# Differential attention with one transposed group split out of PSUM by two engines, a new order of steps, and two small edits in the windowed attention

## The chip, the cores and the metric

The kernel runs on one core of a Trainium2 chip. TensorE (PE; PEld are its weight loads), VectorE (DVE), ScalarE (ACT), GpSimd (POOL) and SyncE (SP, which here only issues DMAs) each run their own instructions in program order and meet through semaphores. The metric is the time of one execution on the device in microseconds (us); lower is better.

## The reference, cut to what matters

One inference step of a two-layer network over 128 context tokens and 1024 latent tokens, all float32. Layer 0 mixes tokens by differential attention, layer 1 by windowed grouped attention with a sink. Each is followed by an output projection and a feed-forward network.

```
# layer 0, latent tokens: 8 heads, 1024 queries, 256 cached + 1024 keys = 1280
s = einsum('bqhmd,bkhmd->bhmqk', q, k) * scale        # m = 0, 1: two score maps per head
p = softmax(s, axis=-1)
a = p[:, :, 0] - lam * p[:, :, 1]
o = einsum('bhqk,bkhe->bqhe', a, v)
# layer 1: 16 heads, blocks of 128 queries, 256 context keys + up to 384 neighbours
s_lat = where(|q_pos - k_pos| <= 128, s_lat, -1e30)
m = maximum(max(s), sink);  e = exp(s - m)
p = e / (sum(e) + exp(sink - m))
```

## The kernel before, in words

**Number format.** Products that need float32 accuracy are made of two rounded halves (float32r): `hi` is the rounded value and `lo` the remainder, and three matmuls (hi hi, hi lo, lo hi) stand for one.

**Differential attention** (`diff_attention`) works on 32 *pairs*: a pair is one head and two blocks of 128 queries (i = 0, 1). Per block and score map m there are 1280 scores. Their way through the engines is cut into steps, each named by a letter:

- S: scores on PE into a PSUM tile (L737, two such tiles). R: row maximum on DVE (L744). E: exponential with row sum on ACT (L749).
- c: the factor of the second map on DVE, a reciprocal (L755) and a product of three columns (L756). C: the combination of both maps, 128x1280, on DVE (L761).
- T: transposes on PE (L768), in groups g = 0, 1, 2 of 4, 4 and 2 blocks of 128 keys, into the one PSUM tile `tpa` (its slot is shared with `tpo`). V: ACT copies the group to SBUF (L773). P: POOL rounds it (`pool_round`, L110) and subtracts the rounded value from it (L784).
- A: products with V on PE (L793 to L795). X, B, Y: the result is copied, transposed back (L806), copied and written to `o_d` (L812).
- W: every other pair, a piece of the output weights is loaded and split on ACT (L102) and DVE (L103).
- l, s, n: loads, statistics and scaling for the first tiles of the output projection that follows (L1253, L1263 and L1275 on ACT).

The order is written out by hand. `ROUND` is a list of tokens run once per pair; a token's letter is the step, its first digits are (g or m, i), and its last digit says how many pairs back it acts. Each engine runs its own instructions in the order in which the tokens emit them. `DRAIN` finishes the last pairs.

**Second attention** (`swa_attention`) has units of one group of four heads and 128 queries. Per head: scores (L1014, L1017, and L1020, which adds the mask by a matmul with the identity), maximum (L1025), its minimum with the negated sink (L1026), exponential (L1029). At its start the mask is loaded by DMA into `mraw` and cast by ACT (L987), and the identity is cast (L989).

Of the kernel before, what the change touches and what calls it, by code (L numbers as in the profile page):

```python
# [9 lines left out]
F32 = mybir.dt.float32  # L10
F32R = mybir.dt.float32r
BF16 = mybir.dt.bfloat16
AF = mybir.ActivationFunctionType
ALU = mybir.AluOpType
# [4 lines left out]
P = 128  # L19
# [25 lines left out]
def hybrid_step(ctx: ExitStack, tc: tile.TileContext, x_prompt, x_sample, cache_diff_k, cache_diff_v,  # L45
# [38 lines left out]
    subg = const.tile([P, 1], F32, name="subg")  # L84
    neglam = const.tile([P, 1], F32, name="neglam")
    negsink = const.tile([P, SH], F32, name="negsink")

    def sbuf(name, side=None):
        return tc.tile_pool(name=name, bufs=1, side=side, reuse_waits="tile")
# [351 lines left out]

    def small_params(sb):

        dma(out=subg, in_=diff_subln_g.rearrange("o p -> p o"))
        act.mul(out=subg, in_=subg, mul=1.0 - LAM_INIT)
        lp = sb.tile([P, 4, HD], F32, name="lp")
        dma(out=lp, in_=diff_lambda.rearrange("o f d -> o (f d)").broadcast_to([P, 4 * HD]).rearrange(
            "p (f d) -> p f d", d=HD))
        lpp = sb.tile([P, 2, HD], F32, name="lpp")
        dve.tensor_tensor(out=lpp, in0=lp[:, 0:4:2, :], in1=lp[:, 1:4:2, :], op=ALU.mult)  # L450
        le = sb.tile([P, 2], F32, name="le")
        dve.tensor_reduce(out=le, in_=lpp, axis=AX.X, op=ALU.add)
        act.activation(out=le, in_=le, func=AF.Exp)
        dve.tensor_tensor(out=neglam, in0=le[:, 1:2], in1=le[:, 0:1], op=ALU.subtract)
        dve.tensor_scalar(out=neglam, in0=neglam, scalar1=-LAM_INIT, scalar2=None, op0=ALU.add)
        dma(out=negsink, in_=swa_sink.broadcast_to([P, SH]))
        act.mul(out=negsink, in_=negsink, mul=-1.0)
# [258 lines left out]
    def diff_attention(op, s1_all, wo_pool, pre, kv0, q0):  # L716
        NKB = NCB + 8
        NK = NKB * P
        with sbuf("da") as sb, psum("dap") as ps:
            class Pair:  # L720
# [31 lines left out]
                def step_c(self, _, i):  # L752

                    r = self.s2[i][:, 1:2]
                    dve.reciprocal(out=r, in_=self.s2[i][:, 0:1])  # L755
                    dve.scalar_tensor_tensor(out=r, in0=self.s1(i), scalar=neglam, in1=r, op0=ALU.mult, op1=ALU.mult)  # L756

                def step_C(self, _, i):

# [4 lines left out]
                def step_T(self, g, i):  # L764

                    tp = self.tp[i, g] = ps.tile([P, 4, P], F32, name="tpa", tag="t", bufs=1)
                    for t in range(4 * g, min(4 * g + 4, NKB)):
                        pe.transpose(tp[:, t - 4 * g, :], self.a[i][:, t * P:(t + 1) * P], ident)  # L768

                def step_V(self, g, i):  # L770
                    n = min(4, NKB - 4 * g)
                    x = self.a32[i, g] = sb.tile([P, 4, P], F32, name="a32", tag="a32", bufs=2)
                    act.copy(out=x[:, 0:n, :], in_=self.tp[i, g][:, 0:n, :])  # L773

                def step_P(self, g, i):

                    n = min(4, NKB - 4 * g)
                    if g not in self.aT:
                        self.aT[g] = sb.tile([P, 2, 4 if g < 2 else 2, 2 * P], F32R, name="aT",
                                             tag="aT" if g < 2 else "aTb", bufs=4 if g < 2 else 2)  # L780
                    hi, lo = [self.aT[g][:, f, 0:n, i * P:(i + 1) * P] for f in range(2)]
                    x = self.a32[i, g][:, 0:n, :]
                    pool_round(hi, x)
                    (dve if self.last else pool).tensor_tensor(out=lo, in0=x, in1=hi.bitcast(F32), op=ALU.subtract)  # L784
# [34 lines left out]
            def wo_piece(i):  # L819
# [5 lines left out]

            ROUND = ("c001 A003 T012 A003 V202 V102 S000 R111 P213 T112 P002 A003 A003 E011 A003 P202 V012 "
                     "C001 P102 E111 T212 R000 V112 W000 S100 P012 R100 T001 X003 A002 V212 c011 E000 A002 "
                     "A002 B003 S010 V001 C011 Y003 T201 R010 A002 P112 E100 A002 T101 S110").split()  # L830


            DRAIN = ("c001 l1 A003 A003 V202 P213 l0 T012 V102 R111 A003 A003 P002 E011 P202 V012 A003 "
# [3 lines left out]
                     "A001 A001 A001 A001 P211 A001 A001 A001 n0 s11 X001 B001 Y001 n1").split()  # L837
            n = len(pairs)

            def run(token, i):  # L840
# [139 lines left out]

    def swa_attention(op, wo_pool, pre, kv0, q0):
        with sbuf("sa") as sb, psum("sap") as ps:

            mask = sb.tile([P, 2, P], BF16, name="mask")
            mraw = sb.tile([P, 2, P], F32, name="mraw")
            dma(out=mraw, in_=swa_mask)
            act.copy(out=mask, in_=mraw)  # L987
            ident_b = sb.tile([P, P], BF16, name="ident_b")
            act.copy(out=ident_b, in_=ident)  # L989

            class Unit:


# [29 lines left out]
                def step_R(self, h):  # L1023
                    hs, nm = self.g * SG + h, self.nm[:, h:h + 1]
                    dve.tensor_reduce(out=nm, in_=self.S[h][:, self.c0:self.c1], axis=AX.X, op=ALU.max, negate=True)  # L1025
                    dve.tensor_tensor(out=nm, in0=nm, in1=negsink[:, hs:hs + 1], op=ALU.min)  # L1026

                def step_E(self, h):
                    act.activation(out=self.e[:, h, 0:self.nk], in_=self.S[h][:, self.c0:self.c1], func=AF.Exp,  # L1029
# [881 lines left out]
    f = la.f  # L1911
# [87 lines left out]
```

## Time and profile before

| | |
|---|---|
| median of 3 runs | 3180.54 us (3177.97 to 3180.6) |
| the profiled execution | 3179.54 us, span of its trace 3177.7 us |
| mean granted TensorE clock | 0.982 of full speed |
| busy share of the span | PE 94%, PEld 83%, DVE 65%, ACT 45%, POOL 38% |

The span runs from the first to the last traced instruction. The shares are means over stages with different limits: the differential attention lies at about 390 to 822 us, the second attention at about 1960 to 2230 us, and the feed-forward and projection stages fill most of the rest.

### The profile page before, as it was taken

Reading aid. Unit: us, or ns where it says so; the run is one execution under the profiler, and the core shown is the slowest. Engines: PE = TensorE matmul, PEld = TensorE weight load, DVE = VectorE, ACT = ScalarE, POOL = GpSimd, SP = SyncE. Lnnn points to the kernel's source line nnn. Section 1 sums busy time; section 2 is a strip of 40 time slices with the busy share of each in tenths; the row PEclk is TensorE's granted clock in tenths of the full one; section 3 lists DMA queues with packets and bytes.
Section 4 is the critical chain, followed back from the end, with each engine's and each line's share of the span. In section 5 each row is a group of like instructions: output and inputs, shape, how many; then the busy total and the mean of one; then the engine's idle time right before and its main releaser. Section 6 shows DMA issues by size and latency. Waiting matters only on the chain.

```text
span 3177.7 us, 47863 instructions
## 1 busy us (share of the span) xinstructions
PE 3000.0 (94%) x17998; PEld 2637.4 (83%) x17998; DVE 2070.7 (65%) x2849; ACT 1423.8 (45%) x2764; POOL 1215.6 (38%) x1120
## 2 busy tenths in 40 slices
PE   8999989988887999999999998999988999999999
PEld 5888777777776999999888787777768999998887
DVE  6786388888587777753786643999586633334544
ACT  6332267777554333333344323777443333333442
POOL 0453389999312444433000143666213434330000
PEclk9999999999898999999999999999999999999999
DMA  6675543332423343424865454433432322226664
GB/s 214 190 222 190 182 135 115 121 115 85 126 100 98 112 125 110 129 83 150 290 215 193 149 174 126 117 114 102 143 116 75 109 67 79 77 70 214 196 197 142
DMA packets 373807, 442.22 MB, mean 139 GB/s; under 512 B 26804, under 2 KB 295644, under 8 KB 373576
## 3 DMA queue, kind: packets, MB, share of 16 engines
q1 hardware_dynamic: 373576, 439.16, 43.9%
q8 instruction: 142, 2.33, 0.3%
q14 instruction: 89, 0.73, 0.1%
HBM read 335.71 MB, written 103.37 MB: 138 GB/s over the span
## 4 chain that ended last, share of the span: by engine, by line
PE 68%; POOL 13%; DVE 9%; ACT 4%; issue 3%; DMA 1%; SPq 1%; ACTq 0%; DVEq 0%; POOLq 0%
POOL aT L784 7%; PE guX L1516 6%; PE guX L1517 6%; PE guX L1518 6%; PE dacc L1633 6%; PE dacc L1635 6%; PE dacc L1634 6%; POOL aT L110 5%; PE qacc L556 4%; PE qacc L558 4%; PE qacc L557 4%; PE guY L1518 3%; PE guY L1516 3%; PE guY L1517 3%; PE guZ L1516 1%
## 5 line engine op out<-in xcount | busy, mean ns | idle before, releaser
L1633 PE MATMUL dacc<-fh,ahl 128*128 128x512 f32 x792 | 311.4, 393 | 2.4 <-DVE U L1552 2.4
L1635 PE MATMUL dacc<-fh,ahl 128*128 128x512 f32 x792 | 310.3, 392 | 0.0
L1634 PE MATMUL dacc<-fl,ahl 128*128 128x512 f32 x792 | 310.3, 392 | 0.0
L1549 POOL TENSOR_TENSOR sg<-sg,U 128x256 f32<-128x256 f32 x88 | 74.9, 851 | 576.2 <-ACT sg L1548 565.0
L556 PE MATMUL qacc<-whi,hh 128*128 128x512 f32 x648 | 259.3, 400 | 0.0
L558 PE MATMUL qacc<-whi,hl 128*128 128x512 f32 x648 | 254.3, 392 | 0.0
L557 PE MATMUL qacc<-wlo,hh 128*128 128x512 f32 x648 | 253.7, 391 | 0.6 <-DVE wlo L106 0.6
L617 POOL TENSOR_TENSOR qout<-t,t 128x512 f32<-128x512 f32 (+1 forms) x56 | 67.8, 1212 | 485.7 <-DVE vst L587 283.5
L784 POOL TENSOR_TENSOR aT<-a,aT 128x512 fp32r<-128x512 f32 x186 | 237.5, 1277 | 15.5
L1618 DVE TENSOR_TENSOR fl<-fraw,fh 128x1024 fp32r<-128x1024 f32 x132 | 161.7, 1225 | 118.6 <-ACT fh L1617 115.0
L744 DVE TENSOR_REDUCE nm<-S 128x1 f32<-128x1280 f32 x128 | 190.2, 1486 | 50.9 <-PE S L737 50.9
L1617 ACT CAST fh<-fraw 128x1024 fp32r<-128x1024 f32 x132 | 138.4, 1049 | 164.0 <-DMA fraw<-in_w_down_dram 157.4
L737 PE MATMUL S<-K,q 128*128 128x512 f32 (+1 forms) x768 | 184.5, 377 | 13.3 <-ACT e L749 9.2
L266 DVE SCALAR_TENSOR_TENSOR macc<-wmod,sc,macc 128x512 f32<-128x512 f32 x196 | 186.3, 994 | 0.0
L1633 PEld LDWEIGHTS dacc<-fh,ahl 128*128 128x128 f32 x792 | 148.7, 188 | 36.4 <-DVE U L1552 3.3
L1635 PEld LDWEIGHTS dacc<-fh,ahl 128*128 128x128 f32 x792 | 148.7, 188 | 33.5
L578 ACT CAST xT<-tpx 128x512 fp32r<-128x512 f32 x127 | 68.8, 591 | 240.2 <-issue 125.4
L1634 PEld LDWEIGHTS dacc<-fl,ahl 128*128 128x128 f32 x792 | 148.7, 188 | 32.8
L749 ACT ACTIVATE e<-S,nm 128x1280 f32<-128x1280 f32 x128 | 171.6, 1340 | 7.2 <-DVE nm L744 7.1
L737 PEld LDWEIGHTS S<-K,q 128*128 128x128 f32 x768 | 137.5, 193 | 44.3 <-ACT e L749 19.5
L110 POOL TENSOR_SCALAR aT<-a 128x512 fp32r<-128x512 f32 x192 | 154.2, 803 | 24.0 <-ACT a L773 24.0
L1488 DVE TENSOR_TENSOR fl<-fsum,fh 128x1024 fp32r<-128x1024 f32 x84 | 102.4, 1219 | 81.0 <-ACT fh L1486 81.0
(363 smaller groups left out, 9592.2 us busy)
## 6 DMA issues: line engine op xcount, KB each, us to landing
fraw<-in_w_down_dram SPq DMA_DIRECT2D x132, 512.0 KB
wmod<-in_w_mod_dram SPq DMA_DIRECT2D x112, 256.0 KB
araw<-a_d SPq DMA_DIRECT2D x132, 192.0 KB
fraw<-in_w_gate_dram SPq DMA_DIRECT2D x44, 512.0 KB
fraw<-in_w_up_dram SPq DMA_DIRECT2D x42, 512.0 KB
qT_d<-xT SPq DMA_DIRECT2D x36, 512.0 KB
q<-qT_d SPq DMA_DIRECT2D x64, 256.0 KB
wraw<-in_w_qkv_diff_dram SPq DMA_DIRECT2D x24, 512.0 KB
```

Of the source, the lines that this page charges most:

```text
L110: pool.tensor_scalar(out=out, in0=in_, scalar1=1.0, scalar2=0.0, op0=ALU.mult, op1=ALU.add)
L556: pe.matmul(acc, lhsT=xh, rhs=hi[:, a, :], start=(kb == 0), stop=False)
L557: pe.matmul(acc, lhsT=xh, rhs=lo[:, a, :], start=False, stop=False)
L558: pe.matmul(acc, lhsT=xl, rhs=hi[:, a, :], start=False, stop=(kb == KB - 1))
L737: pe.matmul(S[:, j:j + n], lhsT=self.q[:, f, m, i * P:(i + 1) * P], rhs=kv[self.h][0][:, m, j:j + n], start=(f == 0), stop=(f == 1))
L784: (dve if self.last else pool).tensor_tensor(out=lo, in0=x, in1=hi.bitcast(F32), op=ALU.subtract)
L1516: pe.matmul(o, lhsT=hi[:, kb, :], rhs=xh[:, kb, :], start=(first and kb == 0), stop=False, **more)
L1517: pe.matmul(o, lhsT=hi[:, kb, :], rhs=xl[:, kb, :], start=False, stop=False, **more)
L1518: pe.matmul(o, lhsT=lo[:, kb, :], rhs=xh[:, kb, :], start=False, stop=(kb == 3), **more)
L1633: pe.matmul(acc, lhsT=ah, rhs=hi[:, cs], start=(d == 0), stop=False)
L1634: pe.matmul(acc, lhsT=ah, rhs=lo[:, cs], start=False, stop=False)
L1635: pe.matmul(acc, lhsT=al, rhs=hi[:, cs], start=False, stop=(d == NDF - 1))
```

## The change

Four edits.

1. In the differential attention, the group g = 2 of block i = 1 (two transposed blocks, 256 columns) no longer goes through SBUF and POOL. ACT casts it from PSUM into `hi`, and DVE subtracts `hi` from the PSUM tile into `lo`. The other five groups of a pair are treated as before.
2. `ROUND` and `DRAIN` are new lists: the same steps in another order.
3. In step c, the product of three columns is a `tensor_scalar` with two column scalars instead of a `scalar_tensor_tensor`.
4. In the second attention, the minimum with the sink is a `tensor_scalar` with a column scalar instead of a `tensor_tensor`; the mask and the identity live in the constant pool and are made in `small_params`, during the first projection.

```diff
     def small_params(sb):
 
+        mraw = junk[:, 0:2 * P].rearrange("p (a k) -> p a k", k=P)
+        dma(out=mraw, in_=swa_mask)
+        act.copy(out=mask, in_=mraw)
+        act.copy(out=ident_b, in_=ident)
...
-                    dve.scalar_tensor_tensor(out=r, in0=self.s1(i), scalar=neglam, in1=r, op0=ALU.mult, op1=ALU.mult)
+                    dve.tensor_scalar(out=r, in0=r, scalar1=self.s1(i), scalar2=neglam, op0=ALU.mult, op1=ALU.mult)
...
+                def halves(self, g, i):
                     n = min(4, NKB - 4 * g)
                     if g not in self.aT:
                         self.aT[g] = sb.tile([P, 2, 4 if g < 2 else 2, 2 * P], F32R, name="aT",
                                              tag="aT" if g < 2 else "aTb", bufs=4 if g < 2 else 2)
+                    return [self.aT[g][:, f, 0:n, i * P:(i + 1) * P] for f in range(2)]
+
+                def step_V(self, g, i):
+
+                    n = min(4, NKB - 4 * g)
+                    if (g, i) == (2, 1):
+                        act.copy(out=self.halves(g, i)[0], in_=self.tp[i, g][:, 0:n, :])
+                        return
+                    x = self.a32[i, g] = sb.tile([P, 4, P], F32, name="a32", tag="a32", bufs=2)
+                    act.copy(out=x[:, 0:n, :], in_=self.tp[i, g][:, 0:n, :])
+
+                def step_P(self, g, i):
+
+                    n = min(4, NKB - 4 * g)
+                    hi, lo = self.halves(g, i)
+                    if (g, i) == (2, 1):
+                        dve.tensor_tensor(out=lo, in0=self.tp[i, g][:, 0:n, :], in1=hi.bitcast(F32), op=ALU.subtract)
+                        return
                     x = self.a32[i, g][:, 0:n, :]
                     pool_round(hi, x)
                     (dve if self.last else pool).tensor_tensor(out=lo, in0=x, in1=hi.bitcast(F32), op=ALU.subtract)
...
-            ROUND = ("c001 A003 T012 A003 V202 V102 S000 R111 P213 T112 P002 A003 A003 E011 A003 P202 V012 "
...
+            ROUND = ("T012 A003 c001 A003 R111 S000 T112 V102 C001 P102 R000 W000 A003 E011 A003 T212 S100 "
...
-            mask = sb.tile([P, 2, P], BF16, name="mask")
-            mraw = sb.tile([P, 2, P], F32, name="mraw")
-            dma(out=mraw, in_=swa_mask)
-            act.copy(out=mask, in_=mraw)
-            ident_b = sb.tile([P, P], BF16, name="ident_b")
-            act.copy(out=ident_b, in_=ident)
...
-                    dve.tensor_tensor(out=nm, in0=nm, in1=negsink[:, hs:hs + 1], op=ALU.min)
+                    dve.tensor_scalar(out=nm, in0=nm, scalar1=negsink[:, hs:hs + 1], scalar2=None, op0=ALU.min)
```

**GpSimd in the steady rounds.** These are ten instructions in a row from the rounds of the differential attention, before; L110 rounds a group (`aT` is the pair of halves, `a_...` the SBUF copy of the group) and L784 subtracts.

```order
L110 TENSOR_SCALAR aT<-a_4553 128x2x128
L784 TENSOR_TENSOR aT<-a_4553,aT 128x2x128
L110 TENSOR_SCALAR aT<-a_4555 128x4x128
L784 TENSOR_TENSOR aT<-a_4555,aT 128x4x128
L110 TENSOR_SCALAR aT<-a_4589 128x4x128
L784 TENSOR_TENSOR aT<-a_4589,aT 128x4x128
L110 TENSOR_SCALAR aT<-a_4604 128x4x128
L784 TENSOR_TENSOR aT<-a_4604,aT 128x4x128
L110 TENSOR_SCALAR aT<-a_4631 128x2x128
L784 TENSOR_TENSOR aT<-a_4631,aT 128x2x128
```

The same stretch of the changed kernel, where L110 has become L113 and L784 has become L802:

```order
L113 TENSOR_SCALAR aT<-a_4722 128x4x128
L802 TENSOR_TENSOR aT<-a_4722,aT 128x4x128
L113 TENSOR_SCALAR aT<-a_4750 128x4x128
L802 TENSOR_TENSOR aT<-a_4750,aT 128x4x128
L113 TENSOR_SCALAR aT<-a_4768 128x4x128
L802 TENSOR_TENSOR aT<-a_4768,aT 128x4x128
L113 TENSOR_SCALAR aT<-a_4794 128x4x128
L802 TENSOR_TENSOR aT<-a_4794,aT 128x4x128
L113 TENSOR_SCALAR aT<-a_4826 128x2x128
L802 TENSOR_TENSOR aT<-a_4826,aT 128x2x128
```

Before, two of the six groups of a pair are the small ones (128x2x128); after, five groups are left and one of them is small.

**VectorE in the steady rounds.** First before: L744 is R, L755 and L756 are c, L761 is C.

```order
L755 RECIPROCAL s_6020<-s_6020 128x1
L756 SCALAR_TENSOR_TENSOR s_6020<-s_all,neglam,s_6020 128x1
L761 SCALAR_TENSOR_TENSOR a<-e,s_6020 128x1280
L744 TENSOR_REDUCE nm<-S 128x1
L755 RECIPROCAL s_6114<-s_6114 128x1
L756 SCALAR_TENSOR_TENSOR s_6114<-s_all,neglam,s_6114 128x1
L744 TENSOR_REDUCE nm<-S 128x1
L761 SCALAR_TENSOR_TENSOR a<-e,s_6114 128x1280
```

Then after, where R is L751, c is L762 and L763, C is L768, and L798 is the new subtraction:

```order
L798 TENSOR_TENSOR aT<-tpa,aT 128x2x128
L762 RECIPROCAL s_5574<-s_5574 128x1
L763 TENSOR_SCALAR s_5574<-s_5574,s_all,neglam 128x1
L751 TENSOR_REDUCE nm<-S 128x1
L768 SCALAR_TENSOR_TENSOR a<-e,s_5574 128x1280
L751 TENSOR_REDUCE nm<-S 128x1
L762 RECIPROCAL s_5626<-s_5626 128x1
L763 TENSOR_SCALAR s_5626<-s_5626,s_all,neglam 128x1
L751 TENSOR_REDUCE nm<-S 128x1
L768 SCALAR_TENSOR_TENSOR a<-e,s_5626 128x1280
L751 TENSOR_REDUCE nm<-S 128x1
```

The new subtraction stands once in a round, behind a row maximum and ahead of a step c; the product in c has become a TENSOR_SCALAR.

**ScalarE at the end of the differential attention.** First before: L773 is V, L800 is X, L810 is Y; L1263 takes the statistics of the output projection's tiles, L1275 their square root, L1312 evicts its first transposes.

```order
L773 COPY a_8330<-tpa 128x256
L1263 ACTIVATE junk,ss_8336<-V 128x128 x4
L810 COPY ot<-tpo 128x256
L1275 ACT_TABLE_LOAD
L1275 ACTIVATE ss_8237<-ss_8237,eps_t 128x8
L1263 ACTIVATE junk,ss_8336<-V 128x128 x4
L800 COPY oT<-av 128x256
L810 COPY ot<-tpo 128x256
L1275 ACTIVATE ss_8336<-ss_8336,eps_t 128x8
L1312 ACTIVATE o_8457<-tp_o,subg 128x512 x2
```

Then after, where X is L818, Y is L828, V of the direct group is L788, statistics L1273, square root L1285 and eviction L1322:

```order
L788 CAST aT<-tpa 128x2x128
L828 COPY ot<-tpo 128x256
L1273 ACTIVATE junk,ss_8278<-V 128x128 x8
L818 COPY oT<-av 128x256
L828 COPY ot<-tpo 128x256
L1273 ACTIVATE junk,ss_8317<-V 128x128 x4
L1285 ACT_TABLE_LOAD
L1285 ACTIVATE ss_8278<-ss_8278,eps_t 128x8
L1273 ACTIVATE junk,ss_8317<-V 128x128 x4
L1285 ACTIVATE ss_8317<-ss_8317,eps_t 128x8
L1322 ACTIVATE o_8398<-tp_o,subg 128x512 x2
```

Before, one square root (L1275) stands between the last Y (L810) and the first eviction (L1312); after, the second tile's eight statistics, the table load and both square roots stand there. On SyncE's queue, the load of the third tile, which before followed the last write of `o_d` directly, comes after two broadcasts and six loads for the prompt's attention.

## Rows read from the trace of the kernel before

**Rows 1.** The page, part 4: shares of the chain that ended last, by engine.
```profile
PE 68%; POOL 13%; DVE 9%; ACT 4%; issue 3%; DMA 1%; SPq 1%; ACTq 0%; DVEq 0%; POOLq 0%
```

**Rows 2.** Windows: stretch, length, busy us (instructions) of PE, PEld, DVE, ACT, POOL, TensorE clock, DMA.
```profile
500.00:757.00 257.00, 231.08 (x1528) 201.43 (x1527) 222.82 (x211) 183.35 (x332) 246.99 (x241) 1.00 0.37 116
2000.00:2200.00 200.00, 187.91 (x1294) 156.78 (x1293) 184.04 (x362) 154.13 (x365) 130.94 (x148) 1.00 0.39 113
```

**Rows 3.** Timeline of SyncE's queue, 575 to 620: start us, us, engine, line, what.
```profile
577.13 0.36 SPq L812 DMA_DIRECT2D o_d<-ot  x1
...
602.71 0.36 SPq L812 DMA_DIRECT2D o_d<-ot  x1
```

**Rows 4.** Groups by line and form, 500 to 757: busy us, mean ns, idle before.
```profile
L784 POOL TENSOR_TENSOR aT<-a,aT 128x512 fp32r<-128x512 f32 x80 | 102.9, 1287 | 6.7
...
L110 POOL TENSOR_SCALAR aT<-a 128x512 fp32r<-128x512 f32 x80 | 78.8, 985 | 0.0
L768 PE MATMUL tpa<-ident,a 128*128 128x128 f32 x402 | 65.8, 278 | 10.0 <-ACT a L773 10.0
...
L784 POOL TENSOR_TENSOR aT<-a,aT 128x256 fp32r<-128x256 f32 x41 | 53.7, 1309 | 3.4
```

**Rows 5.** Timeline 574 to 584: VectorE and GpSimd side by side.
```profile
575.24 0.36 DVE L756 SCALAR_TENSOR_TENSOR s<-s_all,neglam,s 128x1 f32<-128x1 f32 x1
...
575.63 1.66 DVE L761 SCALAR_TENSOR_TENSOR a<-e,s 128x1280 f32<-128x1280 f32 x1
576.04 1.85 POOL L784 TENSOR_TENSOR aT<-a,aT 128x256 fp32r<-128x256 f32 x1
...
579.80 0.41 POOL L110 TENSOR_SCALAR aT<-a 128x256 fp32r<-128x256 f32 x1
...
580.29 0.74 POOL L784 TENSOR_TENSOR aT<-a,aT 128x256 fp32r<-128x256 f32 x1
...
581.00 0.62 POOL L110 TENSOR_SCALAR aT<-a 128x512 fp32r<-128x512 f32 x1
```

**Rows 6.** Single lines in the whole run: count, min/median/max ns, first and last start.
```profile
L756 DVE SCALAR_TENSOR_TENSOR s<-s_all,neglam,s x64: 218/362/633, 402.3 to 801.8; 128x1 f32<-128x1 f32 x64
L784 DVE TENSOR_TENSOR aT<-a,aT x6: 425/687/693, 809.2 to 817.5; 128x512 fp32r<-128x512 f32 x4, 128x256 fp32r<-128x256 f32 x2
L1026 DVE TENSOR_TENSOR nm<-nm,negsink x128: 158/236/1124, 1966.2 to 2223.7; 128x1 f32<-128x1 f32 x128
L755 DVE RECIPROCAL s<-s x64: 145/152/156, 402.1 to 801.6; 128x1 f32<-128x1 f32 x64
L226 DVE TENSOR_SCALAR macc<-wmod,sc x12: 467/480/1517, 116.9 to 305.3; 128x512 f32<-128x512 f32 x12
```

**Rows 7.** Timeline behind the last pair, ScalarE and TensorE.
```profile
818.57 1.28 ACT L1275 ACT_TABLE_LOAD   x1
...
822.35 1.04 PE L1310 MATMUL tp_o<-ident,V 128*128 128x128 f32 x8
...
858.11 1.88 PE L1310 MATMUL tp_o<-ident,V 128*128 128x128 f32 x8 [2.57 <-issue]
```

**Rows 8.** Chain of waits, 815 to 862: start us, us, what.
```profile
817.03 0.41 ACT junk L1263 x2
...
840.11 8.69 DMA V<-o_d
```

**Rows 9.** Chain of waits, 1940 to 1985.
```profile
1961.24 3.44 DMA mraw<-in_swa_mask_dram
```

**Rows 10.** Waits, 1958 to 1985: engine, line, waited for, us in total, times, longest.
```profile
PE S L1020 <- ACT mask L987: 4.7, 1, 4.7
```

**Rows 11.** Timeline of ScalarE in the first projection, 180 to 210.
```profile
199.53 1.08 ACT L578 CAST xT<-tpx 128x512 fp32r<-128x512 f32 x2 [5.09 <-PE tpx L577]
```

**Rows 12.** Chain of waits in the second attention, 1985 to 2200, by line.
```profile
by line: PE tpp L1049 14.3%; DVE nm L1025 12.1%; PE S L1017 8.8%; ACT e L1029 8.4%; DVE nm L1026 8.3%; PE S L1014 8.0%; PE av L1082 6.6%; PE av L1081 6.5%; DVE pT L1072 6.4%; DVE den L1041 3.8%; issue 3.5%; PE S L1020 3.1%; PE tpo L1092 2.0
```

**Rows 13.** Groups by line and form, 2000 to 2200.
```profile
L1026 DVE TENSOR_TENSOR nm<-nm,negsink 128x1 f32<-128x1 f32 x98 | 35.7, 364 | 3.4
```

More of the change, by code (lines that the diff above doesn't have):

```diff
@@ L86, in hybrid_step @@
     negsink = const.tile([P, SH], F32, name="negsink")
+    mask = const.tile([P, 2, P], BF16, name="mask")
+    ident_b = const.tile([P, P], BF16, name="ident_b")
     def sbuf(name, side=None):
@@ L768, in step_T @@
                         pe.transpose(tp[:, t - 4 * g, :], self.a[i][:, t * P:(t + 1) * P], ident)
+                def halves(self, g, i):
+                    n = min(4, NKB - 4 * g)
+                    if g not in self.aT:
+                        self.aT[g] = sb.tile([P, 2, 4 if g < 2 else 2, 2 * P], F32R, name="aT",
+                                             tag="aT" if g < 2 else "aTb", bufs=4 if g < 2 else 2)
+                    return [self.aT[g][:, f, 0:n, i * P:(i + 1) * P] for f in range(2)]
                 def step_V(self, g, i):
                     n = min(4, NKB - 4 * g)
+                    if (g, i) == (2, 1):
+                        act.copy(out=self.halves(g, i)[0], in_=self.tp[i, g][:, 0:n, :])
+                        return
                     x = self.a32[i, g] = sb.tile([P, 4, P], F32, name="a32", tag="a32", bufs=2)
@@ L777, in step_P @@
                     n = min(4, NKB - 4 * g)
[L778 to L781, printed above, removed]
+                    hi, lo = self.halves(g, i)
+                    if (g, i) == (2, 1):
+                        dve.tensor_tensor(out=lo, in0=self.tp[i, g][:, 0:n, :], in1=hi.bitcast(F32), op=ALU.subtract)
+                        return
                     x = self.a32[i, g][:, 0:n, :]
@@ L823, in wo_piece @@
                 wsplit(raw, wo[kb][0][:, cs], wo[kb][1][:, cs])
-            ROUND = ("c001 A003 T012 A003 V202 V102 S000 R111 P213 T112 P002 A003 A003 E011 A003 P202 V012 "
-                     "C001 P102 E111 T212 R000 V112 W000 S100 P012 R100 T001 X003 A002 V212 c011 E000 A002 "
-                     "A002 B003 S010 V001 C011 Y003 T201 R010 A002 P112 E100 A002 T101 S110").split()
-            DRAIN = ("c001 l1 A003 A003 V202 P213 l0 T012 V102 R111 A003 A003 P002 E011 P202 V012 A003 "
[3 rows of a table removed]
-                     "A001 A001 A001 A001 P211 A001 A001 A001 n0 s11 X001 B001 Y001 n1").split()
+            ROUND = ("T012 A003 c001 A003 R111 S000 T112 V102 C001 P102 R000 W000 A003 E011 A003 T212 S100 "
+                     "V012 P012 A002 T001 E111 A002 V112 X003 P112 V212 A002 B003 P212 E000 S010 A002 V001 "
+                     "Y003 T201 A002 A002 c011 R100 P001 T101 C011 E100 R010 V201 P201 S110").split()
+            DRAIN = ("T012 A003 c001 A003 R111 T112 V102 C001 P102 A003 E011 A003 T212 V012 P012 A002 T001 "
[3 rows of a table added]
+                     "A001 X001 B001 Y001 s10 n0 s11 n1").split()
             n = len(pairs)
```

6 rows, old and new, of the table DRAIN are left out of this document.

## The prediction

> **What bounds the kernel now.** I began with the page's chain of waits: TensorE carries 68% of it and POOL 13% [rows 1]. POOL is 38% busy over the span, so its share must come from a few stages in which it is the limit, and the change edits one of them. The windows say which. Between 500 and 757 us, inside the differential attention, POOL is busy 246.99 of 257 us (96%), TensorE 231.08, VectorE 222.82 and ACT 183.35 [rows 2]. To turn this into a price per pair I took SyncE's timeline: the write of a finished pair is issued at 577.13 and, two pairs on, at 602.71 [rows 3], so a pair takes 12.79 us, and 257 us hold 20.09 pairs. Per pair, then: POOL 12.29 us and 0.50 idle, PE 11.50, DVE 11.09, ACT 9.13. POOL sets the period, but PE and DVE follow within 10 to 13%: whatever is taken from POOL can pay at most 1.29 us before PE is full.
>
> POOL's groups by form show why it is full [rows 4]: the subtraction of a four-block group takes 1287 ns and that of a two-block group, half as wide, 1309 ns. The side-by-side timeline explains it [rows 5]: the two-block subtraction that starts at 576.04 takes 1.85 us and ends at 577.89, beside VectorE's combination C (575.63 to 577.29), while the one at 580.29, with no C beside it, takes 0.74. A POOL operation here is held while C runs, and then does its work. The hold lands on whichever POOL instruction is there; it is not saved by removing that one.
>
> In the second attention no engine is full: 187.91 of 200 us for PE, 184.04 for DVE [rows 2]; there the order of waits counts.
>
> **The change, part by part.**
>
> *Group (2, 1) off POOL.* Per round POOL loses one rounding and one subtraction of the small form. Free of holds, the pair runs from 579.80 to the next instruction at 581.00 [rows 5]: 1.20 us. The means with their holds would give more, 1.31 for the subtraction [rows 4] and 0.41 for the rounding, 1.72 in all, but C still runs twice a pair and its hold moves to a neighbour. I take 1.20: POOL's period goes from 12.79 to 11.59. In exchange VectorE gets one subtraction of 256 columns. The same shape ran there for the last pair, all operands in SBUF, in 425 ns [rows 6]; with one operand in PSUM it is new, and I take 0.43 (bounds: 0.4, and 0.69, the duration with twice the columns). ACT casts the same columns as before, into another tile: nothing.
>
> *Step c.* The product took 362 ns in the middle and 218 at best [rows 6]; the long cases wait for POOL, as at 575.24. The `tensor_scalar` form reads one SBUF tensor and two column scalars. An instruction on one column with two tensors cost 158 ns at best (L1026), and the old product, with a scalar more, 218 [rows 6]: a scalar costs about 0.06, so I take 0.27 for two. That frees 2 x 0.09 us of VectorE per pair, which is not the bound: nothing. VectorE ends at 11.09 + 0.43 - 0.18 = 11.34 per pair, beside POOL's 11.59 and PE's 11.50.
>
> *The new order.* It has the same steps. What it must do is keep POOL fed with three engines this close. POOL's rows in the order are an even file, four wide groups and a small one, and nothing there says that it would wait more than now, so I let it keep its 0.50 idle. 31 pairs (the last runs its subtractions on VectorE) x 1.20 = **-37 us**. Bounds: if VectorE's 11.34 alone remained, 31 x 1.45 = -45; the lower end is rival B.
>
> *Tail of the differential attention.* Before, the statistics of the first tiles were interleaved with the last pair, and PE began the projection's transposes at 822.35, as the last pair ended. Now four statistics at some 0.43 (two instructions end to end take 0.41 [rows 8]), a table load of 1.28 [rows 7] and two roots stand behind the last Y on ACT, then VectorE's scaling: I estimate 5 us for the first tile. But PE stood idle for 2.57 us ahead of the fourth tile at 858.11 [rows 7], since that tile's load (840.11, 8.69 us [rows 8]) sits at the end of SyncE's queue, which still starts at the last write of `o_d`. So 2.57 of the 5 are hidden: **+2 us**; bounds 0 and +5. The third tile's load moves behind eight other issues, but PE needs it only two tiles later.
>
> *The mask.* The second attention's first masked scores waited 4.7 us for the cast mask [rows 10], at the end of a 3.44 us load that began at 1961.24 [rows 9]. With both made hundreds of us earlier, that wait goes: **-4.5 us**. What it costs in the first projection is two short casts on ACT, which idles 5.09 us in one gap there [rows 11], and one more DMA issue. If that cover were gone it would be under 1 us.
>
> *Minimum with the sink.* L1026 runs 98 times in the window, 364 ns in the mean [rows 13], 236 in the middle and 158 at best [rows 6]: the spread is waiting for POOL, since both inputs lie in SBUF. It carries 8.3% of the chain over 215 us [rows 12], 17.8 us. With one column scalar in place of the second tensor, one SBUF input is left. An operation of that kind, the reciprocal L755, ran between 145 and 156 ns 64 times beside a POOL that was nearly always busy [rows 6]: never held. I price the new form at 0.16 + 0.06 = 0.21 us: 17.8 x (1 - 0.21/0.364) = **-7.5 us**. Bounds: -10 (0.158 and no hold), and +4 (rival A).
>
> The Trainium skill speaks against this step. Its page "SBUF — State Buffer", section "Who interferes with whom", says that a VectorE instruction with one SBUF input stays clear of GpSimd only outside the 2-port modes, and that `tensor_scalar` can enter those. The wide `tensor_scalar` L226, one SBUF input with a column scalar, agrees: 467 ns at best, 1517 at worst [rows 6]. No row shows one of a single column. By the rule the step would give nothing back.
>
> The sum, against the profiled execution's 3179.54 us (1 us under the median of 3180.54): -37 + 2 - 4.5 - 7.5 = -47, **3132.5 us**.
>
> **The rivals.**
>
> *A. The column `tensor_scalar` is still held by POOL.* Then L1026 keeps its 364 ns of mean and pays 0.06 for the scalar: 128 x 0.06 = 7.7 us if all were on the chain, some half of it, +4. Step c, off the bound, changes nothing. 3132.5 + 7.5 + 4 = 3144. For it: L226's 1517 ns. Against: L755, and that the wide L226 is the nearest row only in its form.
>
> *B. Another engine binds first.* The PSUM slot of `tpa` was freed by ACT's copy, and PE already waited 10.0 us at L768 for that, half a microsecond per pair [rows 4]. For the direct group it is freed only after VectorE's subtraction, 0.43 and its queue later, while PE has 0.09 us of slack in 11.59. PE's period becomes about 11.5 + 0.5 + 0.1 = 12.1: 31 x 0.69 = -21 in place of -37, and 3148.5. For it: PE's 11.50. Against: matmuls overlap and their busy ends are modelled, so PE may have more room, and A steps stand between the direct group and the next use of the slot.
>
> *C. Slower.* VectorE runs in order, and L798 waits for ACT's cast of the same group, which stands behind an exponential and other copies. Every wait w there delays the row maximum behind it, then E, then the S tile that E frees. VectorE's period is 11.34 + w; it passes 12.79 at w = 1.45, and with the other terms' -10 the kernel is slower by 0.2% from w = 1.98. At w = 2.2 it is +23 - 10, 3193. Against: ACT has 3.7 us idle per pair.
>
> *D. More than forecast.* POOL drops the holds too and VectorE's 11.34 binds: -45, no loss at the tail, -10 for the minimum, -4.7: 3120.
>
> **How the numbers follow.** The forecast has 0.46, A 0.20, B 0.23, D 0.05, C 0.03; 0.03 is left for a tail or an order that eats nearly all of it. The range goes from 3119 (D) to 3151 (B and its spread): it leaves out C, the rest and some of B's upper half, under 2 in 10. About 0.2%, 6.4 us, is what a measurement of this kernel can tell from no change. All cases but C and the rest are faster by more: 0.94; within 0.03; slower 0.03.
>
> **What would show it.** In the changed profile: writes of pairs some 11.6 us apart; POOL still 95% busy there with one small group per pair; L798 near 0.43; the product in c under 0.3 and never at 0.36 behind a POOL operation; the minimum (L1036 there) at 0.21 with hardly a spread, or, in A, with maxima over 1 us; no wait for the mask; the gap between the last Y and the first transposes 5 us longer. The prediction is wrong if pairs come 12 us or more apart with POOL idle and PE waiting for VectorE's subtraction, or if VectorE waits in front of L798.

## The result and the profile after

The changed kernel takes 3126.87 us (median of 4 runs, 3125.71 to 3129.43) against 3179.6 us of the kernel before: a ratio of 0.9836, 95% interval 0.9819 to 0.9853. In a second set of four runs, with a kernel before of its own, it took 3126.9 us, 0.9831 [0.9818, 0.9844]. That is 1.6 to 1.7% faster, 53 us; 47 were forecast, and 3132.5 us. The profiled execution has a span of 3127.5 us.

First the page's chain by engine, and the windows of the kernel after, of the differential attention and of the second attention (columns as in [rows 2]).

```profile
PE 71%; POOL 12%; DVE 8%; ACT 4%; issue 2%; DMA 1%; POOLq 0%; ACTq 0%; DVEq 0%; SPq 0%
```

```profile
500.00:740.00 240.00, 233.91 (x1566) 206.19 (x1565) 218.76 (x238) 192.16 (x341) 231.40 (x206) 1.00 0.40 125
1963.00:2149.00 186.00, 180.51 (x1259) 152.60 (x1259) 164.82 (x353) 150.37 (x354) 126.87 (x144) 1.00 0.42 121
```

Against [rows 2], TensorE goes from 90% to 97% busy in the differential attention and POOL stays at 96%: two engines are now full. In the second attention VectorE goes from 92% to 89%, TensorE from 94% to 97%.

The timeline of SyncE's queue, the writes of finished pairs as in [rows 3]:

```profile
575.27 0.36 SPq L830 DMA_DIRECT2D o_d<-ot  x1
...
587.37 0.36 SPq L830 DMA_DIRECT2D o_d<-ot  x1
...
598.62 0.37 SPq L830 DMA_DIRECT2D o_d<-ot  x1
...
621.96 0.36 SPq L830 DMA_DIRECT2D o_d<-ot  x1
```

Four pairs take 46.69 us: 11.67 per pair, where 11.59 was forecast and [rows 3] have 12.79. Rounds with a piece of the output weights take 12.10 and those without it 11.25.

Groups by line and form, 500 to 740 (columns as in [rows 4]; L802 is the subtraction on POOL, L113 the rounding, L798 the new subtraction on VectorE):

```profile
L802 POOL TENSOR_TENSOR aT<-a,aT 128x512 fp32r<-128x512 f32 x83 | 117.9, 1420 | 6.9
...
L113 POOL TENSOR_SCALAR aT<-a 128x512 fp32r<-128x512 f32 x83 | 95.6, 1152 | 0.0
...
L768 DVE SCALAR_TENSOR_TENSOR a<-e,s 128x1280 f32<-128x1280 f32 x42 | 73.1, 1742 | 0.0
L775 PE MATMUL tpa<-ident,a 128*128 128x128 f32 x412 | 67.8, 279 | 2.3 <-DVE aT L798 0.2
...
L802 POOL TENSOR_TENSOR aT<-a,aT 128x256 fp32r<-128x256 f32 x20 | 14.8, 740 | 1.7
...
L798 DVE TENSOR_TENSOR aT<-tpa,aT 128x256 fp32r<-128x256 f32 x21 | 8.8, 418 | 0.0
L113 POOL TENSOR_SCALAR aT<-a 128x256 fp32r<-128x256 f32 x20 | 8.0, 402 | 0.0
```

This is where a hold goes when its victim is removed. Before, a small group cost POOL 1309 ns of subtraction in the mean and a wide one 1287; now the small one runs free at 740 and the wide ones have grown to 1420, their rounding from 985 to 1152 [rows 4]. With 0.41 for the small rounding [rows 5], two small groups at 1.72 became one at 1.14, 2.3 us less per pair, and four wide ones grew by 0.30 each, 1.20 us back: 1.1 us net. That is about the free price of a group (1.20), not the one with its hold. The order changed along with it here; a run further down, in the old order, shows the same.

Single lines in the whole run (columns as in [rows 6]): the minimum, and the product in step c.

```profile
L1036 DVE TENSOR_SCALAR nm<-nm,negsink x128: 211/214/218, 1927.5 to 2172.5; 128x1 f32<-128x1 f32 x128
```

```profile
L763 DVE TENSOR_SCALAR s<-s,s_all,neglam x64: 272/273/277, 403.7 to 770.7; 128x1 f32<-128x1 f32 x64
```

The minimum never takes over 218 ns, where L1026 went up to 1124 [rows 6]. The forecast had 0.21 us for the minimum and 0.27 for the product.

TensorE behind the last pair (compare [rows 7]):

```profile
791.76 1.97 PE L1320 MATMUL tp_o<-ident,V 128*128 128x128 f32 x8 [5.37 <-DVE V L1289]
...
824.73 1.03 PE L1320 MATMUL tp_o<-ident,V 128*128 128x128 f32 x8
```

The first transposes wait 5.37 us, as forecast, and the fourth tile's, which waited 2.57 before, don't wait any more.

### The profile page after: what moved, and what is told of

It is laid out like the page before. It is cut to its first block, busy times and chain, and to the rows that moved or that the text cites. A ratio compares the mean times of both kernels' runs of the same rounds, so it can differ in the third digit from the quotient of the medians.

```text
span 3127.5 us, 47855 instructions
## 1 busy us (share of the span) xinstructions
PE 2988.7 (96%) x17998; PEld 2633.0 (84%) x17998; DVE 2037.3 (65%) x2880; ACT 1432.1 (46%) x2764; POOL 1180.2 (38%) x1057
## 4 chain that ended last, share of the span: by engine, by line
PE 71%; POOL 12%; DVE 8%; ACT 4%; issue 2%; DMA 1%; POOLq 0%; ACTq 0%; DVEq 0%; SPq 0%
POOL aT L802 6%; PE guX L1526 6%; PE guX L1527 6%; PE guX L1528 6%; PE dacc L1643 6%; PE dacc L1645 6%; PE dacc L1644 6%; POOL aT L113 5%; PE qacc L563 4%; PE qacc L565 4%; PE qacc L564 4%; PE guY L1528 3%; PE guY L1526 3%; PE guY L1527 3%; PE guZ L1526 1%
## 5 line engine op out<-in xcount | busy, mean ns | idle before, releaser
L751 DVE TENSOR_REDUCE nm<-S 128x1 f32<-128x1280 f32 x128 | 190.0, 1484 | 33.7 <-PE S L744 32.3
L802 POOL TENSOR_TENSOR aT<-a,aT 128x512 fp32r<-128x512 f32 (+1 forms) x155 | 200.3, 1293 | 12.9
L744 PE MATMUL S<-K,q 128*128 128x512 f32 (+1 forms) x768 | 183.5, 376 | 12.2 <-ACT e L756 11.4
L756 ACT ACTIVATE e<-S,nm 128x1280 f32<-128x1280 f32 x128 | 171.3, 1338 | 12.0 <-DVE nm L751 9.1
L744 PEld LDWEIGHTS S<-K,q 128*128 128x128 f32 x768 | 137.5, 193 | 40.3 <-ACT e L756 15.3
L113 POOL TENSOR_SCALAR aT<-a 128x512 fp32r<-128x512 f32 (+1 forms) x160 | 156.2, 976 | 21.7 <-ACT a L791 21.7
```

What stands on the lines that cost most here:

```text
L113: pool.tensor_scalar(out=out, in0=in_, scalar1=1.0, scalar2=0.0, op0=ALU.mult, op1=ALU.add)
L744: pe.matmul(S[:, j:j + n], lhsT=self.q[:, f, m, i * P:(i + 1) * P], rhs=kv[self.h][0][:, m, j:j + n], start=(f == 0), stop=(f == 1))
```

## The experiments

**The theories.** The prediction's theory: POOL's work sets the period, and 1.20 us less of it is a period shorter by as much, in any sensible order. The rival that concerns this step is B: the direct group holds its PSUM slot until VectorE has subtracted, and TensorE waits. A second question was which of the four edits the 53 us come from. The changed kernel ran once more beside some of them:

> The changed kernel itself, unaltered, run beside the next three so that they can be compared on one chip. 3127 us within 3.

Measured: the 3126.9 us above.

**The direct group alone, in the old order.** On the kernel before, with the new `step_V` and `step_P`, and the token of the direct subtraction placed right behind that of its cast (the same in `DRAIN`):

```diff
-  ROUND = ("c001 A003 ... S000 R111 P213 T112 ... T001 X003 A002 V212 c011 E000 ...
+  ROUND = ("c001 A003 ... S000 R111 T112 ... T001 X003 A002 V212 P212 c011 E000 ...
```

> The kernel before with the direct group alone: group (2, 1) is cast by ScalarE and subtracted by VectorE, in the old order of steps, only with the subtraction placed right behind the cast; mask, minimum and step c are those of before. If POOL's work sets the period of a pair, as the prediction has it, the order matters little: pairs about 11.6 to 11.7 us apart instead of 12.79, and 35 to 38 us less than before. The rival holds that the new order is what lets the other engines keep up: then pairs are 12.1 us or more apart, PE waits for VectorE's subtraction, and the gain is 20 us or less.

Measured: 3203.85 us against 3180.16, a ratio of 1.0073 [1.006, 1.0085]: slower by 24 us. The theory fell where it says "in any sensible order". The waits between 500 and 757 us (engine, line, waited for, us in total, times, longest), and two rounds in the timeline, the first with a split of the output weights (L103), the second without (L781 is the cast, L791 the subtraction, L744 the row maximum):

```profile
POOL aT L110 <- ACT a L784: 55.2, 57, 2.2
...
PE tpa L768 <- DVE s L755: 38.6, 19, 2.1
```

```profile
581.86 0.39 ACT L781 CAST aT<-tpa 128x256 fp32r<-128x256 f32 x1
582.00 1.09 DVE L103 TENSOR_TENSOR wol<-wraw,woh 128x512 fp32r<-128x512 f32 x1
...
583.02 1.48 DVE L744 TENSOR_REDUCE nm<-S 128x1 f32<-128x1280 f32 x1
...
584.42 0.41 DVE L791 TENSOR_TENSOR aT<-tpa,aT 128x256 fp32r<-128x256 f32 x1
...
584.97 0.63 PE L768 MATMUL tpa<-ident,a 128*128 128x128 f32 x4 [2.04 <-DVE s L755]
...
596.04 1.49 DVE L744 TENSOR_REDUCE nm<-S 128x1 f32<-128x1280 f32 x1 [0.90 <-PE S L737]
...
598.01 0.63 PE L768 MATMUL tpa<-ident,a 128*128 128x128 f32 x4 [2.01 <-DVE s L755]
```

The window as in [rows 2], then two rounds from write to write, and two microseconds of the first of them:

```profile
500.00:757.00 257.00, 218.38 (x1429) 199.35 (x1428) 197.80 (x218) 171.74 (x309) 193.91 (x189) 0.95 0.36 113
532.31:546.60 14.29, 12.29 (x77) 11.24 (x76) 10.10 (x11) 8.93 (x17) 11.24 (x11) 0.88 0.21 65
587.33:600.37 13.04, 11.03 (x78) 9.99 (x77) 10.10 (x11) 8.93 (x17) 10.18 (x11) 1.00 0.25 73
544.00:546.00 2.00, 2.00 (x12) 2.00 (x11) 0.75 (x1) 0.52 (x1) 1.31 (x2) 0.50 0.00 0
```

The cast is done at 582.25. The subtraction starts at 584.42, because a split and a row maximum stand ahead of it on VectorE, and TensorE's next transposes wait 2.04 us for the slot. (The wait is put down to L755; the slot's last reader is L791, which ends as TensorE starts again.) The split is not what costs: in the next round, which has none, TensorE waits 2.01 us all the same. There the maximum itself has waited 0.90 us for its scores, so TensorE waits for the maximum of the scores that it has just made (1.49 us) and then for the subtraction (0.41). That happens in each of the 19 rounds, 38.6 us in all, and POOL, now 75% busy, waits in turn for the copies of those transposes. This is rival B, with a wait of 2 us a pair where the prediction had 0.5.

A second loss comes on top of it, from TensorE's clock. Of the 28 rounds between the first write (436.60) and the last of the steady ones (819.24), 12 have a mean granted clock of 0.88 to 0.90 and take 14.37 us in the mean; the other 16 have 0.98 to 1.00 and take 13.14. In the round that begins at 532.31, TensorE has waited 2.00 us for the slot, and then the clock falls: between 544 and 546 it is 0.50, the lower of its two levels (1.2 GHz), as it is for some 3 us in each of the 12. In the round from 587.33, which has such a wait too, it stays at 1.00; why only some rounds lose it isn't shown. In the kernel before, the changed kernel and the traces of all the other orders it is 1.00 throughout this stage. By the two means, 31 rounds without the lowered clock would be some 16 us shorter, the larger part of the 24 us.

**The new order alone.** On the kernel before, only `ROUND` and `DRAIN` of the change.

> The kernel before with the new order of steps alone; all six groups still go through POOL. If POOL's work is the bound, the pairs stay 12.79 us apart, the tail behind the last pair costs 1 to 2 us, and the time is that of before within 3 us. The rival holds that the order by itself shortens the period: then 10 us or more are gained without any work taken from POOL.

Measured: 3180.44 against 3180.16, 1.0002 [0.9993, 1.0011]. Its window:

```profile
500.00:757.00 257.00, 230.83 (x1521) 201.15 (x1520) 221.73 (x211) 186.21 (x330) 247.00 (x241) 1.00 0.37 116
```

POOL is busy 247.00 of 257 us, as in [rows 2]. The order by itself gives nothing, and the direct group put into the old order as it stood costs 24 us.

**What in the old order is in the way.** The first experiment again, with the two steps that stood ahead of the subtraction moved behind it:

```diff
-  ... T212 R000 V112 W000 S100 P012 R100 T001 X003 A002 V212 P212 c011 E000 ...
+  ... T212 R000 V112 S100 P012 T001 X003 A002 V212 P212 W000 R100 c011 E000 ...
```

> The direct group in the old order once more, with two steps moved: the split of the output weights (W) and the row maximum R100 come behind VectorE's subtraction instead of ahead of it; TensorE's order is the old one. In the run before, the cast was ready at 582.25 us and the subtraction began at 584.42, behind a split and a maximum, and TensorE waited 38.6 us in 19 rounds for the slot. If that queue alone made the old order slow, the wait falls below 5 us, pairs come 11.7 to 12.2 us apart, and 20 to 38 us are gained on the kernel before. The rival: the old order is too tight elsewhere too, since the maximum now comes later; then pairs stay above 12.6 us.

Measured: 3153.89 us against 3180.34, 0.9915 [0.99, 0.993]: 26 us faster than before, and 50 us faster than the same kernel with two steps elsewhere. In the profiled execution (the fastest, 3143.95 us) the writes of pairs, the wait for the slot and POOL's two forms of subtraction (500 to 740) are:

```profile
583.59 0.36 SPq L823 DMA_DIRECT2D o_d<-ot  x1
...
630.04 0.36 SPq L823 DMA_DIRECT2D o_d<-ot  x1
```

```profile
PEld tpa L768 <- DVE aT L791: 3.6, 20, 0.2
```

```profile
L795 POOL TENSOR_TENSOR aT<-a,aT 128x512 fp32r<-128x512 f32 x84 | 131.5, 1566 | 7.0
...
L795 POOL TENSOR_TENSOR aT<-a,aT 128x256 fp32r<-128x256 f32 x21 | 15.5, 737 | 1.8
```

Four pairs take 46.45 us, 11.61 each, as short as in the changed kernel, and the clock stays at 1.00. So the two steps ahead of the subtraction made the old order slow, and by the waits above, with and without a split, the maximum is the one of them that counts. The hold moved in the old order too: the small subtraction runs free at 737 ns, and the wide one has grown from 1287 to 1566. But this kernel's five runs lie between 3143.95 and 3159.25, a spread of 15 us where the other kernels have 2 to 7; what its slower executions do was not traced and stays open. With the mask and the minimum (4 and 12.6 us, below) its gain makes 43 of the 53 us by the median and all of them by the fastest execution. How much the rest of the new order gives is therefore open as well.

**Both small groups direct.** In the changed kernel, `(g, i) == (2, 1)` becomes `g == 2` in both steps, with the order as it is; and then with the second group's steps moved forward.

```diff
-  ... A002 c011 R100 P001 T101 C011 E100 R010 V201 P201 S110
+  ... A002 c011 R100 P001 V201 P201 T101 C011 E100 R010 S110
```

> The changed kernel with the other small group of a pair, (2, 0), also cast by ScalarE and subtracted by VectorE, in the same order of steps. POOL loses another 1.15 us per pair. In the trace after, POOL is 96% and TensorE 97% busy. If TensorE is the next bound, pairs go from 11.67 to 11.4 us or so, and 5 to 9 us are gained. The rival: the PSUM slot of the group is freed later, behind what VectorE has queued ahead of the subtraction, as it was in the old order; then pairs are 12 us or more apart and 10 us or more are lost against the changed kernel.

> Both small groups of a pair direct, as in the run that was slower than the changed kernel by 23 us, but with the second one's cast and subtraction moved ahead of the combination C011 and the exponential E100. In that run a cast was done at 586.82 us and its subtraction began at 587.28, behind a row maximum, and TensorE waited 15.2 us for it in 240. If this queue is all, pairs come 11.3 to 11.7 us apart and the time is 3115 to 3128. The rival: two groups that hold the slot for two engines are too much for TensorE wherever they stand; then pairs stay above 12 us and the time above 3140.

Measured: 3149.58 us, 0.9905 [0.9891, 0.9918], with the order as it is, and 3175.39, 0.9991 [0.9982, 1.0], with the steps moved; the changed kernel's own ratio is 0.9831. By the writes of `o_d`, pairs come 12.41 and 13.26 us apart, as both rivals had it. The waits of the first between 500 and 740:

```profile
POOL aT L113 <- ACT a L791: 40.1, 29, 2.1
...
PE tpa L775 <- DVE aT L798: 15.2, 20, 0.9
```

and of the second, with its subtraction in the timeline:

```profile
DVE aT L798 <- ACT aT L788: 47.9, 27, 2.6
...
PEld tpa L775 <- DVE aT L798: 7.4, 18, 0.4
```

```profile
597.10 0.42 DVE L798 TENSOR_TENSOR aT<-tpa,aT 128x256 fp32r<-128x256 f32 x1 [2.64 <-ACT aT L788]
```

In the first, TensorE waits for the subtraction as in the old order, and its rival is right in the reason too. In the second the rival has the numbers but not the reason: TensorE hardly waits for the subtraction. It comes too early for its cast: VectorE stands still 2.64 us in front of it, 47.9 us in 27 times, with the combination and the next maximum queued behind. That is the mechanism of rival C. A direct group asks for a place in VectorE's order that is neither behind long instructions nor ahead of its cast. Whether a third place would suit two such groups was not tried.

**The split out of the way.** In the changed kernel, a split still stands right ahead of the subtraction in every other round. Here it is moved:

```diff
-  ROUND = ("T012 A003 c001 A003 R111 S000 T112 V102 C001 P102 R000 W000 A003 E011 ...
+  ROUND = ("T012 A003 c001 W000 A003 R111 S000 T112 V102 C001 P102 R000 A003 E011 ...
```

> The changed kernel with one step moved: the split of a piece of the output weights (W, every other round) comes right behind step c001, where VectorE waits 0.8 to 1.1 us for scores, and no longer right ahead of the direct group's subtraction. In the trace after, rounds with a split take 12.1 us and rounds without it 11.27; in one of them the cast was ready at 583.83 us and the subtraction began at 584.62, behind 1.08 us of the split. If it is the queue ahead of the subtraction, rounds with the split fall to 11.3 to 11.6 us and 8 to 13 us are gained against the changed kernel's 3127. The rival: POOL, 96% busy, and TensorE, 97%, leave no room, or the row maximum behind the split is late instead; then the time stays within 4 us of 3127.

Measured: 3129.39 us, 0.984 [0.9827, 0.9854], the changed kernel's time. The writes of pairs, and the window as in [rows 2]:

```profile
575.63 0.36 SPq L830 DMA_DIRECT2D o_d<-ot  x1
...
587.45 0.36 SPq L830 DMA_DIRECT2D o_d<-ot  x1
...
598.96 0.37 SPq L830 DMA_DIRECT2D o_d<-ot  x1
```

```profile
500.00:740.00 240.00, 234.52 (x1566) 206.56 (x1565) 223.15 (x238) 192.88 (x340) 231.50 (x205) 1.00 0.40 125
```

Rounds with the split fell from 12.10 to 11.82 and the others rose from 11.25 to 11.51: two rounds take 23.33 us, where they took 23.35. The wait at the subtraction was not what the period hung on; POOL's 231.50 us of 240 are the same to a tenth in both kernels. That fits the rival, by which the two full engines leave no room; which of the two sets the period was not separated.

**The minimum alone, the mask alone.** On the kernel before, edit 4's two halves apart.

> The kernel before with the minimum of the second attention as a tensor_scalar alone. The prediction priced this at -7.5 us, by the share of the chain; the trace after shows the second attention some 12 us shorter from its first to its last product with V. If the minimum alone did that, since VectorE and the waits of ScalarE behind it were nearly full, 11 to 13 us are gained here. The rival: the minimum gives its 7.5, and the rest belongs to the earlier mask and the clock at the start; then 6 to 9 us.

> The kernel before with the mask and the identity made early, alone. The wait of 4.7 us for the mask goes: 3.5 to 4.7 us are gained. The rival: the extra load and casts in the first projection cost the 1.6 us by which the differential attention began later in the trace after; then 2 to 3 us.

Measured: the minimum 3167.57 us, 0.9959 [0.9946, 0.9971], 12.6 us less than before; the mask 3176.18 us, 0.9988 [0.9979, 0.9997], 4 us less. The interval of the mask, 1 to 7 us, takes in the rival's 2 to 3 as well. But no matmul waits for the mask in that trace, and the differential attention begins at 392.2 us there and at 391.7 in the second trace of the changed kernel (391.9 before), so the later start of 393.5 us in the trace after was not the mask's doing. For the minimum, first the products with V in the second attention of before (first to last start), then the same line and the waits for the minimum, before and with it (1985 to 2220):

```profile
L1082 PE MATMUL av<-pT,V x152: 387/397/500, 1979.0 to 2232.1; 128*128 128x512 f32 x152
```

```profile
L1082 PE MATMUL av<-pT,V x152: 387/397/501, 1978.2 to 2219.2; 128*128 128x512 f32 x152
```

```profile
ACT e L1029 <- DVE nm L1026: 47.7, 43, 2.6
PEld S L1014 <- ACT e L1029: 21.7, 22, 1.9
```

```profile
ACT e L1029 <- DVE nm L1026: 37.5, 37, 1.7
...
PEld S L1014 <- ACT e L1029: 11.6, 12, 1.2
```

From the first product to the last it is 253.1 us before and 241.0 with the minimum alone (241.1 in the changed kernel): the mask has no part in that. ScalarE waits 10 us less for the minimum, and TensorE 10 us less for ScalarE.

**Step c put back.** The changed kernel with `scalar_tensor_tensor` in step c again.

> The changed kernel with step c's product put back to the scalar_tensor_tensor of two tensors. The prediction priced the new form at nothing, since VectorE is not the bound: then 3127 us within 3. The rival: in the tight new order the product's wait for POOL (0.36 us, sometimes 0.6, in place of 0.273) delays the combination behind it and the holds of POOL; the trace after shows the combination at 1742 ns where it had 1989. Then 5 us or more are lost.

Measured: 3125.78 us, 0.9832 [0.9819, 0.9845], as without it. The line in the whole run:

```profile
L763 DVE SCALAR_TENSOR_TENSOR s<-s_all,neglam,s x64: 218/219/606, 401.4 to 766.9; 128x1 f32<-128x1 f32 x64
```

In the new order the old form hardly ever meets POOL (219 ns in the middle, against 362 in [rows 6]) and is then shorter than the 273 of the new one. The edit changes the time by nothing that can be measured.

**The tail.** The changed kernel, with the first tile's statistics and root moved into ScalarE's gaps:

```diff
-  ... E111 A002 V112 X003 P112 V212 A002 B003 P212 A002 V001 Y003 l1 l0 T201 ...
+  ... E111 A002 l1 l0 V112 X003 P112 V212 s00 A002 B003 P212 A002 V001 Y003 T201 ...
-  ... V211 A001 B002 P211 A001 Y002 s00 s01 A001 ... X001 B001 Y001 s10 n0 s11 n1
+  ... V211 s01 A001 B002 P211 A001 Y002 n0 A001 ... X001 B001 Y001 s10 s11 n1
```

> The changed kernel, with the statistics of the output projection's first tile and its square root moved ahead of the last X in the drain, into the gaps in which ScalarE waits for transposes. In the trace after, TensorE stands idle for 5.37 us between the last pair and the projection's first transposes. If those statistics are the cause, the idle time falls to about 1 to 2 us, the last write leaves 1 to 1.5 us earlier, and 1.5 to 4 us are gained against the changed kernel. The rival: the fourth tile's load at the end of SyncE's queue decides; then 1.5 us at most, and TensorE waits there instead.

Measured: 3125.78 us, 0.9828 [0.9815, 0.9842]: not to be told from the changed kernel. TensorE's timeline:

```profile
786.71 1.09 PE L1320 MATMUL tp_o<-ident,V 128*128 128x128 f32 x8 [0.37 <-DVE V L1289]
794.32 1.94 PE L1320 MATMUL tp_o<-ident,V 128*128 128x128 f32 x8 [6.51 <-issue]
...
823.81 1.03 PE L1320 MATMUL tp_o<-ident,V 128*128 128x128 f32 x8
```

The 5.37 us of waiting shrink to 0.37, and 6.51 come back one tile later, where the second tile's statistics now stand in the way. The fourth tile starts 0.9 us earlier and, against the rival, doesn't wait.

**One column and two.** Behind each minimum of the changed kernel, one more instruction, whose result isn't used:

```diff
+  dve.tensor_scalar(out=scr, in0=negsink[:, 0:2], scalar1=negsink[:, hs:hs + 1], scalar2=None, op0=ALU.min)
```

> The changed kernel with one more instruction behind each minimum of the second attention: the same tensor_scalar with a column scalar, on two columns of a table in SBUF instead of one; its result isn't used. On one column it took 211 to 218 ns in all 128 cases. If the form on two columns can be held by POOL, as the wide one was (467 to 1517 ns), its longest case is over 700 ns and the median above 300. The rival: it takes 0.21 to 0.23 us always, and only wide ones are held.

Its two lines in the whole run, the minimum and the addition:

```profile
L1037 DVE TENSOR_SCALAR nm<-nm,negsink x128: 211/214/217, 1917.8 to 2181.2; 128x1 f32<-128x1 f32 x128
```

```profile
L1038 DVE TENSOR_SCALAR scr<-negsink x128: 217/236/1334, 1918.0 to 2181.3; 128x2 f32<-128x2 f32 x128
```

The form on two columns is held, up to 1334 ns; that on one column never is, in the same stretch. The expected median of over 300 ns did not come: it is 236, so that most of the 128 are held little or not at all. The time was 3134.62 us in a single run.

## Why the prediction was right, step by step

**The sum.** By the prediction's terms, with what was measured:

| term | forecast | measured |
|---|---|---|
| pairs of the differential attention | -37 | -38 |
| tail behind it | +2 | +1 to +3 |
| mask | -4.5 | -4 |
| minimum with the sink | -7.5 | -12.6 |
| step c | 0 | 0 |
| together | -47 | -53 |

The pairs: from the first row maximum to the last write 431.0 us before (391.9 to 822.9) and 393.3 after (393.5 to 786.8). This is not quite the forecast's sum come true. By its own formula, 31 rounds times the measured 1.12 us (12.79 less 11.67), the steady rounds give 35. The other 3 us come from the first and last pairs, a term that the prediction didn't have: the new order alone already takes 427.6 us there (393.3 to 820.9) with the period unchanged. That the smaller gain per round and the unforeseen one at the ends make up for each other is luck. Nearly all of the 6 us by which the forecast fell short belong to the minimum. The tail: from the last write, the fourth tile's transposes start after 37.9 us instead of 35.2, the fifth's after 51.95 (838.75) instead of 50.8 (873.72).

**The direct group.** The price, 1.20 us per round and no more, because holds move to the neighbour, is borne out by the groups by form above. VectorE's subtraction was 0.42 us (0.43 forecast). The prediction had VectorE at 11.34 us per pair; it is 218.76 of 240, 10.64, mostly since the combination, too, waits less (1742 ns; 73.1 us for 42).

**The new order.** Here the working was too short. "It has the same steps" and POOL's even file of groups were taken to mean that POOL would be fed. That came true, but the reason given did not carry it, and here the forecast was lucky: the same file in the old order starves POOL. What decides is where the direct subtraction stands in VectorE's order, between the end of its cast and TensorE's next use of the slot. The rival B named this, and put the wait at 0.5 us a pair; in an order not made for it, it is 2 us. No rival had the fall of TensorE's clock that came with it there. The new order brings the wait to almost nothing: TensorE's at L775 is 2.3 us in all in 240, where it was 10.0 in 257 [rows 4].

**The minimum.** The mechanism was right, and so was the duration: 0.21 us, never held. The term that was mis-sized is the one that scaled the chain's 17.8 us by the durations. 128 instructions became shorter by 0.15 us in the mean, 19 us; the chain credited 7.5 of them, and 12.6 came. The likely reason, which no run shows by itself: VectorE was 92% busy there, and a minimum that is not on the chain of one execution still delays the next maximum on the same engine. Here the gain lay between the chain's share and the total.

**The mask, step c, the tail** came as forecast, the mask within a wide interval. That the tail is covered at the fourth tile is supported by the experiment on it: moving 5 us of work there moved the result by less than could be measured.

**The rivals.** A did not occur: the one-column form is not held. The Trainium skill's rule against it stands in "SBUF — State Buffer", "Who interferes with whom": a `tensor_scalar` can enter a 2-port mode, which contends, when its operands meet the conditions of that mode. The prediction left this condition out. Another page of the Trainium skill, "VectorE: DVE Perf Modes", section "Mode 2×_2P — use both read ports for one tensor", asks that the outermost dimension that is not one be even, or odd and equal in source and destination. A single column, as we read it, has no such dimension, and the runs agree: 211 to 218 ns on one column, 217 to 1334 on two and 467 to 1517 on 512 [rows 6]. B and C both exist, and were seen when the order was wrong. D was not reached: POOL is still full, and TensorE now beside it.

## What to carry to other kernels

When work is moved off a full engine onto two others, count its free duration as the gain, since here the hold by another engine only moved to the next instruction. Then look at what stands ahead of the moved instruction in its new engine's order, because a buffer that it frees is late by all of that, and at what those instructions wait for in turn. An edit and its place in the order are one change: here the new order alone gave nothing, the direct group in the old order lost 24 us, the two together gave some 36, and moving only two steps of the old order had already given 26. When an engine begins to wait, look at its granted clock too: the larger part of those 24 us was not the wait itself. The share of a chain is not the whole of what shorter instructions give on a nearly full engine: here the chain said 7.5 us, the instructions lost 19, and 12.6 came.

## What the hardware showed unexpectedly

A `tensor_scalar` on one column and one on two columns differ by 6 ns at their shortest (211 and 217), and by over a microsecond at their longest beside POOL (218 and 1334): only the second is held. A `scalar_tensor_tensor` on one column with two tensors takes 218 ns free, less than the `tensor_scalar` with two column scalars, 273.

With the direct group in the old order, TensorE waited 2 us once a round, and behind 12 of 28 such waits its granted clock fell to 0.50 for some 3 us. Those rounds took 1.2 us longer than the others (14.37 against 13.14).
